# A DiT block pair on one Trainium2 core: a written order around the router, and a first gather for two expert pairs

## The chip, the cores and the metric

The kernel runs on one core of a Trainium2 chip. The core has five engines with instruction streams of their own: TensorE (PE) for matmuls, VectorE (DVE), ScalarE (ACT), GpSimd (POOL) and SyncE (SP), which here issues most of the weight loads. Sixteen DMA engines move the data. The metric is the device time of one execution in microseconds, the median of several runs.

## The reference

Two layers of a diffusion transformer work on 256 positions of x and 256 of a context, D = 1024, all in float32. Both layers take shift, scale and gate rows from a conditioning vector (`adaln`: a 1024 x 6144 matrix per layer). Layer 0 mixes with a gated linear attention and a spatial gating unit, projects back with `w_out` and ends with a mixture of experts on all 512 rows; layer 1 is a latent attention with the same mixture on the 256 rows of x. Around the change the layer reads:

```python
x = x + gate * (mix @ w_out)                     # residual of the mixer
h = modulate(rmsnorm(x, g), shift, scale)        # input of the router and of the experts
logits = h @ w_r + b_r                           # 4 group logits, 4 x 8 expert logits
# one softmax over groups and a top-2 softmax inside the chosen group: two experts per row
x = x + gate * sum_e weight_e * (silu(h Wg_e) * (h Wu_e)) Wd_e      # 32 experts, M_FF = 512
```

The gated linear attention, the latent attention and the rotary angles are not touched and are left out here.

## The kernel before

512 rows are four tiles of 128 tokens, `xs[0..3]` (0 and 1 are x, named `xx`; 2 and 3 the context, named `w` in the trace). A float32 product is done as three products of rounded halves, `mm3` (lines 120 to 122): a high and a low part of each operand, made by `split` (ACT copies the high part at line 115, DVE subtracts at line 116).

**Output projection (pool `out0`).** The mixer's result is multiplied with `w_out` in two halves of 512 columns. For the second half the loop `for t in range(4)` splits the weight into `WH` and `WL` (only at t = 0), does the 24 matmuls of tile t, and adds the gated result to `xs[t]` (`residual`, lines 776 and 777). `ada_next` computes a chunk of the conditioning rows of layer 1: 32 matmuls (L399, x64 in the trace) with 4 for the bias (L407), an ACT copy, and four small DMAs from the POOL queue into the DRAM tensor `mod`. Four chunks are left when the projection's second half begins.

**Router.** `R.half` and `R.tile` take the sum of squares, the inverse root (`rsqrt`, lines 95 to 101), turn the tile with 8 transposes (L213), and form 40 logits with 8 matmuls (L217) and one DVE instruction (L218, `lg`). `R.rows` makes the modulated rows: DVE multiplies with the broadcast row `rA` (L229), POOL adds the broadcast row `rS` (L230), then `split` writes them as `hH0`, `hL0`, `hH1`, `hL1`. `rA` and `rS` are 512 KB broadcast loads from `mod`, two of each, issued from ACT's queue. `R.route(0, 3)` and then `R.route(3, 4)` choose the experts: a chain of some forty small DVE steps (lines 248 to 302) that makes the mask `Mb`, PE's prefix sums over tokens (L277, L279), the positions `cm` (L281) and the weights `wsel`.

All engines but PE in the experts' part follow a scheduler that takes the ready instruction of highest priority; the order it finds is fixed in each engine's stream. On the projection PE too is ordered by it.

**Experts (`moe`).** Experts are handled in 16 pairs, up to 64 rows for each expert. For two pairs at a time, a one-hot matrix `P` (L856, 128 x 4 tiles x 256) selects the rows: `gather` (L881) multiplies the tokens with `P` and writes `xT`, transposed rows. A step of one pair is: two gate-and-up products (L916, `gu`, 16 matmuls for each expert; a float32 matmul is two in the trace, so x64 for both), `hidden` on ACT and DVE, `turned` (L935), `back` (L901), `down` (L1027, `dn`), and, delayed by a step, `combine` (L1046), which puts results back. PE runs this under a written order (`tc.manual_schedule`). The first gather is for one pair (128 columns of `P`); the other 128 columns are gathered inside step 0, between the second `gu` and `turned`. Later gathers are for two pairs at once, 256 columns. Between the first gather and the first `gu` stand four matmuls of `R.blocks` (L309), which lead to the count `nx` (L316), whose value SP reads before it goes on with loads; an overflow loop, which is not entered here, depends on it.

The weights of the experts, 12 MB a pair, come in 1 MB pieces through SP's queue (L849) into 13 buffers in layer 0 and 17 in layer 1; a load waits until PE has finished with what its buffer held.

Of the kernel before, what the change touches and what calls it, by code (L numbers as in the profile page):

```python
# [6 lines left out]
F32 = mybir.dt.float32  # L7
# [18 lines left out]
def body(ctx, tc, I, out, dbg=None, stop=None):  # L26
# [60 lines left out]
    def rsqrt(ss, n, inv, base=None):  # L87
# [9 lines left out]
        act(y, y, AF.Exp, scale=-0.5)  # L97
        V.tensor_tensor(a, y, y, op=OP.mult)
# [39 lines left out]
    class Router:  # L138
# [63 lines left out]
        def tile(self, t):  # L202

            cp, Q, c = self.cp, self.Q, t // 2
            ss = sm.tile([128, 1], F32, name="ss", bufs=4)
            act(junk_of(512), xs[t][:, 512:1024], AF.Square, accum_out=ss)
            rstd = rsqrt(ss, 1, 1.0 / D, self.v0[:, t:t + 1])
# [7 lines left out]
            pl = Q("bt")  # L215
# [3 lines left out]
            return rstd  # L219

        def rows(self, t, rstd, hs, A=None, S=None):
# [11 lines left out]
            split(h2, hs[:, 0, :], hs[:, 1, :])  # L233

        def route(self, t0, t1):
# [38 lines left out]
            prk = Q("bt", (128, 4, 32))  # L274
            for i in range(NT):
                t = t0 + i
                mm(prk[:, i, :], before, Mb[:, t, :], start=i == 0, stop=t == 0, skip_group_check=True)  # L277
                for u in range(t):
                    mm(prk[:, i, :], ones, Mb[:, u, :], start=False, stop=u == t - 1, skip_group_check=True)  # L279
            cm = self.cm[:, ts]  # L280
            V.scalar_tensor_tensor(cm, prk[:, 0:NT, :], 1.0, Mb[:, ts], op0=OP.add, op1=OP.mult)  # L281

            ge = small([4], "gex")
            V.tensor_tensor(ge, lg[:, :, 0:4], m1[:, :, 0:1].to_broadcast([128, NT, 4]), op=OP.subtract)
            act(ge, ge, AF.Exp)
            gs, gmax = small([1], "gs"), small([1], "gmax")
            V.tensor_reduce(gs[:, :, 0], ge, axis=AX.X, op=OP.add)
            V.tensor_reduce(gmax[:, :, 0], ge, axis=AX.X, op=OP.max)
            V.reciprocal(gs, gs)
            V.tensor_tensor(gs, gs, gmax, op=OP.mult)  # L290
            w1, w2, hw = small([5], "w1"), small([5], "w2"), small([5, 8], "l3")
            V.tensor_tensor(w2, m2, m1, op=OP.subtract)
            act(w2, w2, AF.Exp)
            V.tensor_scalar(w1, w2, 1.0, None, op0=OP.add)
            V.reciprocal(w1, w1)
            V.tensor_tensor(w1, w1, gs.to_broadcast([128, NT, 5]), op=OP.mult)
            V.tensor_tensor(w2, w1, w2, op=OP.mult)
            for h, w in ((hb, w1), (h2, w2)):
                src = h1 if h is hb else h2
                V.tensor_tensor(h.rearrange("p t g e -> p (t g) e"), src.rearrange("p t g e -> p (t g) e"),  # L300
                                w.rearrange("p t g -> p (t g)")[:, :, None].to_broadcast([128, NT * 5, 8]), op=OP.mult)
            V.tensor_tensor(fl(hw), fl(hb), fl(h2), op=OP.add)
            chosen(self.wsel[:, ts], hw)
# [28 lines left out]
    def even_layer(HL, main):  # L332
# [6 lines left out]
        with ExitStack() as st:  # L339
# [53 lines left out]
            def ada_chunk(l, c, w, cols=None):  # L393

                g, half = divmod(c, 2)
                pa = P("ad")
                for k in range(KC):
                    for j in range(4):
                        mm(pa[32 * j:32 * j + 32, 0:128], cst[:, k, :], w[k // 4][:, k % 4, j * 128:(j + 1) * 128],  # L399
                           start=k == 0, stop=cols is not None and k == KC - 1, skip_group_check=True)  # L400
                r = ap.tile([128, 128], F32, name="ada_r", bufs=2)
                if cols is not None:
                    act(r, pa[:, 0:128], AF.Copy)
                    tp(cols[:, c, :], r, ident)
                    return
                for j in range(4):
                    mm(pa[32 * j:32 * j + 2, 0:128], sbi[:, l * 12 + c, :], adab[:, j * 128:(j + 1) * 128],  # L407
                       start=False, stop=True, skip_group_check=True)
                if (l, g) in gains:
# [76 lines left out]
            def ada_next():  # L486
                ada_chunk(*adaq.pop(0))
                ada_ahead()
# [274 lines left out]
        with ExitStack() as st:  # L763
# [20 lines left out]
            rows, w, WH, WL = {}, ahead[0], [], []  # L784
            for t in range(4):
                c = t // 2
                if t % 2 == 0:
                    rows[c] = (bcast_row(cp, mod[0, 4, c], D, "rA"), bcast_row(cp, mod[0, 3, c], D, "rS"))
                acc = P("mm")
                for k in range(KC):  # L790
# [4 lines left out]
                    mm3(acc, tok(cH, k, t), tok(cL, k, t), WH[k], WL[k], k == 0, k == KC - 1)  # L795
                R.half(t)
                residual(t, 1, acc)
                rstd = R.tile(t)
                if t == 3:
                    R.route(0, 3)  # L800
                    R.route(3, 4)
                R.rows(t, rstd, HL.tile([128, 2, D], F32R, name=("hH0", "hL0", "hH1", "hL1")[t]), *rows[c])
# [7 lines left out]
    def moe(R, wxa, nwb, out=None):  # L810
# [5 lines left out]
        with ExitStack() as st:  # L816
# [301 lines left out]
            def step(p):  # L1118
# [70 lines left out]
    def odd_layer(HL, main):  # L1189
        rs = main.enter_context(tc.tile_pool(name="rs1", bufs=1, reuse_waits="tile"))  # L1190
        with ExitStack() as st:
# [194 lines left out]
            with tc.tile_pool(name="rt1", bufs=1, reuse_waits="tile") as R.cp, \  # L1386
# [35 lines left out]
                R.route(0, 2)  # L1422
# [57 lines left out]
```

## Time and profile before

| | us |
|---|---|
| median of 3 runs | 1553.11 |
| lowest, highest | 1551.04, 1554.37 |
| the profiled execution | 1554.18 |
| its span in the trace | 1552.40 |
| PE busy | 1459.8 (94%) |
| DVE, ACT, POOL busy | 664.9, 434.0, 225.3 |

The profile is of one execution. Its time is 1.78 us more than the span in the trace. Times in the trace count from the span's start. PE is busy for 94% of the span, but that is not the same as saying that PE sets the end: in parts it runs at half clock, and in parts the transfers set the pace. The stages are: projections and the mixer of layer 0 up to about 330 us, the second half of the output projection with the router up to 389, the experts of layer 0 from 389 to about 899, the latent attention up to 1075, and the experts of layer 1 to the end. The clock column of a window gives the granted TensorE clock as a share of 2.4 GHz; 0.50 is 1.2 GHz.

### The profile page before, as it was taken

How to read it: one execution, taken by the hardware profiler on the slowest of the kernel's cores; microseconds unless marked ns; L12 is line 12 of the kernel's file. 1: busy time of each engine (PE TensorE's matmuls, PEld its weight loads, DVE VectorE, ACT ScalarE, POOL GpSimd, SP SyncE). 2: the span in 40 equal slices, each digit the busy share in tenths (PEclk: the TensorE clock that was granted, in tenths of full speed). 3: DMA queues.
4: the chain of work that ended last, by engine and by line, in shares of the span. 5: the costliest groups of instructions: out<-in, count | busy, mean ns of one | idle time of the engine just before them, and what ended most of it. 6: DMA issues, size and time to landing. Idle time of an engine off the chain costs nothing. (4 is left out here: it accounts for less than half of the span.)

```text
span 1552.4 us, 21816 instructions
## 1 busy us (share of the span) xinstructions
PE 1459.8 (94%) x8622; PEld 857.8 (55%) x8622; DVE 664.9 (43%) x1498; ACT 434.0 (28%) x988; POOL 225.3 (15%) x250
## 2 busy tenths in 40 slices
PE   7999999998999999999999988997999989989987
PEld 5777777867644554554535356786344434444443
DVE  4555556758224334244413455576232332322222
ACT  4433334623121121111112144453222212212212
POOL 2321212133002112012203221101010100010010
PEclk9999999998799999999999989997999999999999
DMA  9774434885899999999999853125999999999994
GB/s 356 232 256 143 156 120 161 299 318 192 320 372 420 420 420 420 420 420 420 382 376 382 321 216 112 43 96 204 372 420 420 420 419 421 420 420 421 420 420 191
DMA packets 126052, 495.24 MB, mean 319 GB/s; under 512 B 17739, under 2 KB 38636, under 8 KB 77816
## 3 DMA queue, kind: packets, MB, share of 16 engines
q1 hardware_dynamic: 119704, 487.33, 79.6%
q10 hardware_dynamic: 2192, 3.72, 0.7%
q0 software_dynamic: 4048, 2.73, 0.6%
q8 instruction: 71, 1.16, 0.3%
q14 instruction: 37, 0.30, 0.1%
HBM read 492.59 MB, written 1.13 MB: 318 GB/s over the span
## 5 line engine op out<-in xcount | busy, mean ns | idle before, releaser
L916 PE MATMUL gu<-w,xT 128*64 128x512 f32 x2048 | 462.9, 604 | 18.0 <-DMA w<-in_moe_w_gu_dram 13.2
L916 PEld LDWEIGHTS gu<-w,xT 128*64 128x64 f32 x2048 | 153.3, 139 | 316.9 <-issue 278.5
L1027 PE MATMUL dn<-w,hh 128*64 128x512 f32 x960 | 219.5, 604 | 0.0
L924 DVE COPY hh<-gu 128x256 f32<-128x256 f32 x64 | 27.2, 425 | 371.3 <-ACT junk L923 371.3
L1050 POOL TENSOR_TENSOR xx<-xx,z 128x512 f32<-128x512 f32 x56 | 72.9, 1324 | 767.4 <-DVE z L1049 767.4
L1027 PEld LDWEIGHTS dn<-w,hh 128*64 128x64 f32 x960 | 76.1, 139 | 121.9 <-issue 112.3
L923 ACT ACTIVATE junk<-gu 128x256 f32<-128x256 f32 x64 | 24.6, 384 | 401.7 <-PE gu L916 401.7
L120 PE MATMUL mm<-WH,hH 128*128 128x512 f32 x288 | 116.7, 407 | 0.8 <-ACT hH L115 0.7
L121 PE MATMUL mm<-WL,hH 128*128 128x512 f32 x288 | 115.2, 400 | 1.4 <-DVE WL L116 1.4
L122 PE MATMUL mm<-WH,hL 128*128 128x512 f32 x288 | 112.5, 400 | 0.0
L1017 DVE SCALAR_TENSOR_TENSOR y<-dn,ws,y 128x512 fp32r<-128x512 f32 x60 | 45.0, 751 | 145.7 <-ACT y L1016 143.6
L1046 PE MATMUL ad<-y,PT 128*128 128x512 f32 x368 | 94.8, 404 | 5.3 <-DVE z L1049 4.1
L1016 ACT ACTIVATE y<-dn,ws 128x512 fp32r<-128x512 f32 x60 | 41.2, 687 | 176.1 <-PE dn L1027 165.6
L1046 PEld LDWEIGHTS ad<-y,PT 128*128 128x128 f32 x368 | 66.0, 188 | 36.1 <-issue 13.0
L115 ACT ACTIVATE WH<-w 128x512 fp32r<-128x512 f32 x80 | 48.4, 627 | 107.6 <-PE mm L122 86.0
L116 DVE TENSOR_TENSOR WL<-w,WH 128x512 fp32r<-128x512 f32 x76 | 56.6, 752 | 50.9 <-ACT WH L115 49.4
L1049 DVE TENSOR_TENSOR z<-ad,gt 128x512 f32<-128x512 f32 x100 | 66.1, 683 | 13.3 <-PE ad L1046 10.2
L881 PE MATMUL ad<-P,hH 128*128 128x256 f32 (+1 forms) x288 | 63.0, 302 | 1.5 <-DVE P L856 1.5
L120 PEld LDWEIGHTS mm<-WH,hH 128*128 128x128 f32 x288 | 54.9, 191 | 16.9 <-issue 3.8
L399 PE MATMUL ad<-w,cst 128*32 128x128 f32 x1536 | 59.3, 280 | 5.1 <-DMA w<-in_ada_w_dram 5.0
L121 PEld LDWEIGHTS mm<-WL,hH 128*128 128x128 f32 x288 | 54.8, 190 | 13.1 <-DVE WL L116 1.5
L122 PEld LDWEIGHTS mm<-WH,hL 128*128 128x128 f32 x288 | 54.5, 191 | 13.2 <-issue 1.6
(434 smaller groups left out, 1989.3 us busy)
## 6 DMA issues: line engine op xcount, KB each, us to landing
w<-in_moe_w_gu_dram SPq DMA_DIRECT2D x256, 1024.0 KB, 16.3
w<-in_moe_w_dn_dram SPq DMA_DIRECT2D x120, 1024.0 KB, 12.0
w<-in_ada_w_dram SPq DMA_DIRECT2D x48, 1024.0 KB, 7.4
w<-in_ev_w_in_dram SPq DMA_DIRECT2D x32, 256.0 KB, 4.6
w<-in_moe_w_dn_dram SPq DMA_DIRECT2D x16, 512.0 KB, 11.2
w<-in_ev_w_in_dram SPq DMA_DIRECT2D x6, 1024.0 KB, 5.1
w<-in_ev_w_out_dram SPq DMA_DIRECT2D x4, 1024.0 KB, 6.8
w<-in_od_w_out_dram SPq DMA_DIRECT2D x4, 1024.0 KB, 5.0
```

What stands on the lines that cost most here:

```text
L115: act(H, src, AF.Copy)
L116: (eng or V).tensor_tensor(L, src, H, op=OP.subtract)
L120: mm(out, lh, rh, start=start, stop=False, skip_group_check=True)
L121: mm(out, lh, rl, start=False, stop=False, skip_group_check=True)
L122: return mm(out, ll, rh, start=False, stop=stop, skip_group_check=True)
L399: mm(pa[32 * j:32 * j + 32, 0:128], cst[:, k, :], w[k // 4][:, k % 4, j * 128:(j + 1) * 128], start=k == 0, stop=cols is not None and k == ...
L881: mm(px[:, j, :], hs[t][:, part, 256 * (k // 2) + k % 2:256 * (k // 2) + 256:2], P[:, t, :], start=i == 0, stop=i == 2 * NT - 1)
L916: mm(gu[64 * c:64 * c + 64, :], xT[:, k, base:base + CAP], w[:, c], start=k == 0, stop=k == KC - 1)
L1027: mm(py[c][64 * par:64 * par + 64, :], hT[par][:, k // 2, k % 2, :], w_[par][:, k % 2, c * 512:(c + 1) * 512], start=k == 0, stop=k == 3)
L1046: mm(cb, PT[:, t, :], y[c][:, i % 2], start=i == 0, stop=i == 2 * len(pend) - 1)
L1049: V.tensor_tensor(z, cb, gate[t // 2][:, hs_], op=OP.mult)
L1050: (V if n % 4 == 3 else nc.gpsimd).tensor_tensor(xs[t][:, hs_], xs[t][:, hs_], z, op=OP.add)
```

## The change

1. From the projection's second half to the placement of the rows (`place`), PE, DVE and ACT run in a written order. The tile loop is cut into pieces: `project(t, k0, k1)` does half of a tile's 24 matmuls, `R.square`, `R.turn`, `R.logits` and the generator `R.rows` are called one by one. The four conditioning chunks, cut into `ada_chunk` (PE) and `ada_out` (the copy and the DMAs), get fixed places.
2. The addition of `rS` goes from POOL to DVE (line 245 of the changed kernel), and `rA` and `rS` are issued from POOL's queue in place of ACT's.
3. `route(0, 3)` and `route(3, 4)` become one `choose(0, 4)`, `place(0, 4)`, and `rest()`, which computes the weights. Layer 1 gets `choose(0, 2)`, `place` and `rest` too.
4. The first gather takes all 256 columns of `P`, and the gather inside step 0 is gone, in both layers. The making of `P` gets a high priority.

The core of the diff:

```diff
-            nc.gpsimd.tensor_tensor(h2, h2, S, op=OP.add)
+            yield
+            V.tensor_tensor(h2, h2, S, op=OP.add)
+            def mod_rows(c):
+                rA[c], rS[c] = (bcast_row(cp, mod[0, i, c], D, n, eng=nc.gpsimd) for i, n in ((4, "rA"), (3, "rS")))
...
+            mod_rows(0)
+            rstd, rows, xT = {}, {}, {}
+            with tc.manual_schedule(engines={mybir.EngineType.PE, mybir.EngineType.DVE, mybir.EngineType.Activation}):
+                project(0, 0, 4)
+                sums = ada_chunk(*adaq.pop(0))
+                project(0, 4, KC)
+                R.half(0)
+                ada_out(*sums)
+                ada_ahead()
+                for t in range(4):
+                    if t < 3:
+                        R.half(t + 1)
+                        if t < 2:
+                            project(t + 1, 0, 4)
+                    residual(t, 1, acc[t])
+                    if t:
+                        rows[t - 1] = rows_of(t - 1)
+                        next(rows[t - 1])
+                    ss = R.square(t)
+                    rstd[t] = rsqrt(ss, 1, 1.0 / D, R.v0[:, t:t + 1], (lambda: next(rows[t - 1])) if t else None)
+                    if t == 3:
+                        R.logits(2, rstd[2], xT[2])
+                    xT[t] = R.turn(t)
+                    if t:
+                        next(rows[t - 1])
+                        next(rows[t - 1], None)
+                    if t == 2:
+                        mod_rows(1)
+                    if t < 2:
+                        project(t + 1, 4, KC)
+                        R.logits(t, rstd[t], xT[t])
+                        if t == 1:
+                            sums = ada_chunk(*adaq.pop(0))
+                            ada_ahead(wpa)
+                            project(3, 0, 4)
+                            ada_out(*sums)
+                    elif t == 2:
+                        project(3, 4, KC)
+                rows[3] = rows_of(3)
...
+                rest = R.choose(0, 4)
+                next(rows[3])
+                next(rows[3], None)
+                R.place(0, 4)
...
+            rest()
...
-                elif p == 0:
-                    gather(P[:, :, 128:256], xT[:, :, 128:256])
...
-            P = one_hots(0)
+            with tc.high_priority():
+                P = one_hots(0)
...
-                gather(P[:, :, 0:128], xT[:, :, 0:128])
+                gather(P, xT)
```

What the diff leaves open is how the streams stand after it. On PE, where the second half of the projection begins, the stream before reads (`one` belongs to a column sum for the router, `w,cst` and `adab,sbi` to the conditioning chunks, `WH`, `WL` to the projection):

```order
L399 MATMUL ad<-w,cst 32x128 x32
L407 MATMUL ad<-adab,sbi 2x128 x4
L190 MATMUL bt<-s_3408,one 128x40
L399 MATMUL ad<-w,cst 32x128 x32
L120 MATMUL mm<-WH_3450,hH_3070 128x512
L407 MATMUL ad<-adab,sbi 2x128 x2
L120 MATMUL mm<-WH_3450,hH_3070 128x512
L407 MATMUL ad<-adab,sbi 2x128 x2
L190 MATMUL bt<-s_3417,one 128x40
L121 MATMUL mm<-WL_3451,hH_3070 128x512
```

And in the changed kernel, from the same place to the middle of tile 0:

```order
L192 MATMUL bt<-s_3408,one 128x40
L192 MATMUL bt<-s_3417,one 128x40
L122 MATMUL mm<-WH_3452,hH_3070 128x512
L123 MATMUL mm<-WL_3453,hH_3070 128x512
...
L123 MATMUL mm<-WL_3474,hH_3070 128x512
L124 MATMUL mm<-WH_3473,hL_3072 128x512
L434 MATMUL ad<-w,cst 32x128 x32
L437 MATMUL ad<-adab,sbi 2x128 x4
L122 MATMUL mm<-WH_3517,hH_3070 128x512
```

The two chunks that stood in front of the projection are gone from there: one now stands in the middle of tile 0, the next between tiles 2 and 3, the last two behind the logits of tile 3. Both column sums stand ahead of the first projection matmul.

On DVE, the end of the router before (the second chain, of tile 3 alone, with the numbers 383x to 387x) and the making of `P`:

```order
L264 TENSOR_TENSOR hb_3837<-h_3839,h_3847 128x40
L297 TENSOR_TENSOR w_3871<-w_3870,w_3871 128x5
L269 TENSOR_TENSOR Mb<-hb_3837,h_3839 128x32
L300 TENSOR_TENSOR h_3847<-h_3847,w_3871 128x40
L300 TENSOR_TENSOR hb_3837<-h_3839,w_3870 128x40
L302 TENSOR_TENSOR l_3872<-hb_3837,h_3847 128x40
L281 SCALAR_TENSOR_TENSOR cm<-bt,Mb 128x32
L269 TENSOR_TENSOR wsel<-l_3872,h_3839 128x32
L856 TENSOR_TENSOR P<-iota,cm 128x1024
```

In the changed kernel, the last logits and the additions of `rS` in front of the chain, and what stands between `Mb` and `P`:

```order
L251 TENSOR_TENSOR hH_3823<-h_3824,hH_3823 128x1024
L243 SCALAR_TENSOR_TENSOR h_3866<-w,rs_y,rA 128x1024
L233 SCALAR_TENSOR_TENSOR lg<-bt,rs_y,bS_3418 128x40
L245 TENSOR_TENSOR h_3866<-h_3866,rS 128x1024
L288 TENSOR_REDUCE m_3959<-lg 128x20
...
L298 TENSOR_TENSOR Mb<-hb_3962,h_3964 128x32 x4
L251 TENSOR_TENSOR hL_3865<-h_3866,hL_3865 128x1024
L322 TENSOR_TENSOR h_3972<-h_3972,w_4014 128x160
L322 TENSOR_TENSOR hb_3962<-h_3964,w_4013 128x160
L262 SCALAR_TENSOR_TENSOR cm<-bt,Mb 128x128
L324 TENSOR_TENSOR l_4015<-hb_3962,h_3972 128x160
L298 TENSOR_TENSOR wsel<-l_4015,h_3964 128x32 x4
L946 TENSOR_TENSOR P<-iota,cm 128x1024
```

One chain over 160 elements stands where two chains, of 120 and of 40, ran into each other. The addition of `rS` for tile 3 stands ahead of the chain, and the subtraction of `split` between `Mb` and `cm`.

On PE, from the first gather to the second pair, before:

```order
L881 MATMUL ad<-P,hH_3705 128x128 x2
L881 MATMUL ad<-P,hL_3883 128x128 x2
...
L309 MATMUL bt<-Mb,ones 128x32
L916 MATMUL gu<-w,xT 64x512 x32
L881 MATMUL ad<-P,hH_3551 128x128 x2
L881 MATMUL ad<-P,hL_3625 128x128 x2
```

and in the changed kernel, up to the first `gu` of the second pair:

```order
L971 MATMUL ad<-P,hL_3865 128x256 x2
...
L333 MATMUL bt<-Mb,ones 128x32
L1006 MATMUL gu<-w,xT 64x512 x32
L1025 MATMUL bt<-ident,hh 128x128 x4
L991 MATMUL bt<-ident,z 128x128 x4
L1117 MATMUL dn<-w,hh 64x512 x16
L1006 MATMUL gu<-w,xT 64x512 x32
```

The 64 matmuls of the first gather have 256 columns in place of 128, and the 64 that stood between the second `gu` and `turned` (L935 before, L1025 now) are gone; nothing stands in their place. On POOL's queue the issues of `rA` and `rS` stand, for the first pair, ahead of the additions of the first residual half, and for the second pair behind the `mod` writes of the first two chunks.

## Rows read from the trace of the kernel before

**Rows 1.** Page, part 4: the chain that ended last, by line, in its second row.

```profile
DMA w<-in_moe_w_gu_dram 9%; DMA w<-in_moe_w_dn_dram 5%; PE gu L916 1%; PE dn L974 0%; PE dn L1027 0%; PE ad L1046 0%; PE ad L958 0%; DVE xT L992 0%; PE bt L134 0%; DVE hh L927 0%; PE ad L961 0%; ACT xT L998 0%; PE bt L935 0%; DVE z L1033 0%; PE ad L988 0%
```

**Rows 2.** Windows: stretch, length, busy time by engine, granted clock, DMA share, GB/s.

```profile
390.00:400.00 10.00, 10.00 (x49) 10.00 (x49) 0.69 (x1) 0.00 (x0) 0.54 (x1) 0.50 0.93 385
400.00:410.00 10.00, 10.00 (x47) 5.08 (x48) 1.61 (x5) 0.60 (x1) 0.00 (x0) 0.75 0.34 109
...
440.00:500.00 60.00, 59.77 (x312) 29.46 (x308) 22.85 (x37) 11.42 (x26) 8.17 (x6) 1.00 1.01 420
...
1080.00:1090.00 10.00, 10.00 (x43) 6.18 (x45) 2.97 (x9) 1.83 (x4) 0.00 (x0) 0.62 0.06 18
```

**Rows 3.** Waits of SP's queue from 400 to 800 us: total, times, longest.

```profile
SPq L849 <- PE dn L1027: 178.3, 25, 12.8
```

**Rows 4.** Timeline of PE, start of the projection's second half and its end.

```profile
330.49 1.96 PE L399 MATMUL ad<-w,cst 128*32 128x128 f32 x64
...
338.69 0.51 PE L121 MATMUL mm<-WL,hH 128*128 128x512 f32 x1 [1.38 <-DVE WL L116]
...
365.64 0.39 PE L121 MATMUL mm<-WL,hH 128*128 128x512 f32 x1
365.86 0.40 PE L122 MATMUL mm<-WH,hL 128*128 128x512 f32 x1
```

**Rows 5.** Timeline of DVE, the modulated rows of tiles 0 and 1.

```profile
355.77 1.28 DVE L229 SCALAR_TENSOR_TENSOR h<-xx,rs_y,rA 128x1024 f32<-128x1024 f32 x1
...
357.16 3.46 DVE L229 SCALAR_TENSOR_TENSOR h<-xx,rs_y,rA 128x1024 f32<-128x1024 f32 x1
```

**Rows 6.** Timeline of DVE, from the last logits to the one-hot matrix.

```profile
380.38 0.25 DVE L218 SCALAR_TENSOR_TENSOR lg<-bt,rs_y,bS 128x40 f32<-128x40 f32 x1
380.55 0.27 DVE L248 TENSOR_TENSOR h<-l,m 128x120 f32<-128x120 f32 x1
...
387.43 1.22 DVE L856 TENSOR_TENSOR P<-iota,cm 128x1024 fp32r<-128x1024 f32 x1
```

**Rows 7.** DMA issues from 340 to 440 us: queue, count, size, median time to landing.

```profile
gt<-mod POOLq DMA_DIRECT2D x2, 512.0 KB, 7.8
```

**Rows 8.** Timeline of PE, first gather to the second pair's gate-and-up.

```profile
388.70 0.69 PE L881 MATMUL ad<-P,hH 128*128 128x128 f32 x2 [1.54 <-DVE P L856]
...
402.69 15.09 PE L916 MATMUL gu<-w,xT 128*64 128x512 f32 x64
...
427.34 7.09 PE L1027 MATMUL dn<-w,hh 128*64 128x512 f32 x32
434.26 2.31 PE L916 MATMUL gu<-w,xT 128*64 128x512 f32 x10
```

**Rows 9.** Window inside a later gather, instructions of L881 alone (PE, PEld, clock, DMA).

```profile
508.00:514.00 6.00, 5.75 (x48) 5.58 (x47) 1.00 1.02 421
```

**Rows 10.** Timeline of PE, a run of 256-column matmuls in the latent attention.

```profile
948.28 0.58 PE L121 MATMUL mm<-wL,kvH 128*128 128x256 f32 x1 [0.37 <-POOL wL L116]
...
950.79 0.41 PE L120 MATMUL mm<-wH,kvH 128*128 128x256 f32 x1
...
951.91 0.28 PE L122 MATMUL mm<-wH,kvL 128*128 128x256 f32 x1
```

**Rows 11.** Timeline of PE, the first pair behind the overflow check.

```profile
787.94 0.51 PE L935 MATMUL bt<-ident,hh 128*128 128x128 f32 x2
...
792.94 9.35 PE L1027 MATMUL dn<-w,hh 128*64 128x512 f32 x32
802.12 1.45 PE L916 MATMUL gu<-w,xT 128*64 128x512 f32 x6
```

**Rows 12.** Timeline of PE, first gather and first pair of layer 1.

```profile
1077.37 7.09 PE L881 MATMUL ad<-P,s 128*128 128x128 f32 x32 [1.43 <-DVE P L856]
...
1084.47 3.94 PE L916 MATMUL gu<-w,xT 128*64 128x512 f32 x10
```

**Rows 13.** Window of the projection of tile 0 with a low clock.

```profile
340.20:343.40 3.20, 3.20 (x9) 2.50 (x8) 3.20 (x8) 0.00 (x0) 2.02 (x4) 0.50 1.07 421
```

More of the change, by code (lines that the diff above doesn't have):

```diff
@@ L214, in tile, with logits @@
                 act(xT[:, kk * 4:kk * 4 + 4, :], p, AF.Copy)
-            pl = Q("bt")
+            return xT
+        def logits(self, t, rstd, xT):
+            c, pl = t // 2, self.Q("bt")
             for k in range(KC):
@@ L272, in route @@
             chosen(Mb[:, ts], hb)
[L274 to L291, printed above, removed]
@@ L305, in blocks @@
+            return rest
         def blocks(self, cp, Q):
@@ L399, in ada_chunk, with ada_sums @@
                         mm(pa[32 * j:32 * j + 32, 0:128], cst[:, k, :], w[k // 4][:, k % 4, j * 128:(j + 1) * 128],
-                           start=k == 0, stop=cols is not None and k == KC - 1, skip_group_check=True)
+                           start=k == 0, stop=k == KC - 1, skip_group_check=True)
                 r = ap.tile([128, 128], F32, name="ada_r", bufs=2)
[L402 to L405, printed above, removed]
+                act(r, pa[:, 0:128], AF.Copy)
+                tp(cols[:, c, :], r, ident)
+            def ada_sums(l, c, w, pa):
+                for k in range(KC):
+                    for j in range(4):
+                        mm(pa[32 * j:32 * j + 32, 0:128], cst[:, k, :], w[k // 4][:, k % 4, j * 128:(j + 1) * 128],
+                           start=k == 0, stop=False, skip_group_check=True)
                 for j in range(4):
@@ L408, in ada_chunk, with ada_out @@
                        start=False, stop=True, skip_group_check=True)
+                return l, c, pa
+            def ada_out(l, c, pa):
+                g, half = divmod(c, 2)
+                r = ap.tile([128, 128], F32, name="ada_r", bufs=2)
                 if (l, g) in gains:
@@ L783, in even_layer, with project @@
                 residual(t, 0, acc0[t])
[L784 to L790, printed above, removed]
+            w, WH, WL, acc = ahead[0], [], [], {}
+            rA, rS = {}, {}
+            def mod_rows(c):
+                rA[c], rS[c] = (bcast_row(cp, mod[0, i, c], D, n, eng=nc.gpsimd) for i, n in ((4, "rA"), (3, "rS")))
+            def project(t, k0, k1):
+                if k0 == 0:
+                    acc[t] = P("mm")
+                for k in range(k0, k1):
                     if t == 0:
@@ L794, in even_layer @@
                         split(w[k // 4][:, k % 4, :], WH[k], WL[k])
[L795 to L802, printed above, removed]
+                    mm3(acc[t], tok(cH, k, t), tok(cL, k, t), WH[k], WL[k], k == 0, k == KC - 1)
@@ new lines, in rows_of @@
+            def rows_of(t):
+                return R.rows(t, rstd[t], HL.tile([128, 2, D], F32R, name=("hH0", "hL0", "hH1", "hL1")[t]), rA[t // 2], rS[t // 2])
+            mod_rows(0)
[38 more added lines that the diff above has]
+                next(rows[3])
+                sums = ada_chunk(*adaq.pop(0)) if adaq else None
+                R.logits(3, rstd[3], xT[3])
+                next(rows[3])
+                if sums:
+                    ada_out(*sums)
+                    sums = ada_chunk(*adaq.pop(0)) if adaq else None
+                rest = R.choose(0, 4)
+                next(rows[3])
+                next(rows[3], None)
+                R.place(0, 4)
+                if sums:
+                    ada_out(*sums)
@@ L803, in even_layer @@
+            assert not adaq and not todo
+            rest()
             while adaq:
@@ L1421, in odd_layer @@
                     rstds.append(R.tile(t))
-                R.route(0, 2)
+                rest = R.choose(0, 2)
+                R.place(0, 2)
+                rest()
                 for t in range(2):
-                    R.rows(t, rstds[t], HL.tile([128, 2, D], F32R, name=f"s{t}"))
+                    for _ in R.rows(t, rstds[t], HL.tile([128, 2, D], F32R, name=f"s{t}")):
+                        pass
         return R
```

69 lines of the change are left out of this document (50 added, 19 removed).

## The prediction, made before the changed kernel ran

> **What bounds the kernel now.** I read the windows by stage first, then the waits of the load queue, then the chain that ended last, and only then the timelines of the places that the change touches.
>
> In the experts of layer 0 PE is busy 59.77 of 60 us at full clock, beside a DMA share of 1.01 [rows 2]. Both look full, and the queue's waits decide: from 400 to 800 us SP waits 178.3 us for `dn` matmuls, that is, for buffers that PE still holds [rows 3]. So PE sets the pace there, and a microsecond saved on PE before 440 moves the whole stage, provided the loads can come earlier too. They can: from 400 to 410 the DMA share is only 0.34 [rows 2], and 13 buffers are filled ahead. In layer 1 the chain that ended last is the weight loads, with every PE line at 1% or less [rows 1]. There a saving on PE counts only where it starts the stream earlier; the stream stands nearly still from 1080 to 1090, at a share of 0.06 [rows 2].
>
> The stretch of the change itself lies on one path: projection, last logits, choice, `P`, first gather, first pair. From 390 to 400 PE is 10.00 of 10.00 busy, and so is its weight load, but the clock is 0.50 [rows 2]: 1.2 GHz. The first gather takes from 388.70 to 402.69, with four small matmuls 13.99 us, and the first `gu` begins at that clock [rows 8].
>
> **The written order up to `P`.** Before, the first projection matmul with `WL` comes at 338.69, after a wait for DVE, and tile 3 ends at 366.26; two chunks of 1.96 us (about 2.35 with their bias matmuls) stand ahead of it [rows 4]. Now these two stand inside, 4.7 us; the start gains less, since the order waits for both column sums and for DVE's first `WL`: I estimate 337.1 for the start, so tile 3 ends 3.1 us later, at 369.4.
>
> Behind it the path is shorter. Before, the last logits come at 380.38, 14.1 us after the projection, and `P` starts 7.05 us later [rows 6]. Part of these 14.1 us is contention: one DVE instruction with `rA` takes 1.28 us alone and 3.46 when POOL adds `rS` beside it [rows 5]. With the addition on DVE, four instructions of about 1.2 us come onto DVE, 4.9 us, but those stretched by POOL shrink: 2.2 us for the one of tile 1. Counting the instructions of the new DVE order with 1.2 to 1.3 us for each of 128x1024, 0.3 for each 160-wide step (0.27 at 120 wide [rows 6]) and 0.1 for small ones: 1.4 for the residual, 1.3 + 1.2 for tile 2's row, 1.2 + 1.3 for its split and tile 3's product, 0.3 + 1.2 for logits and addition, 5.1 for the chain up to `Mb`, 2.6 for the subtraction, weights and `cm`, 1.2 for `P`: 16.8, and 1.8 for waits on ACT between them. `P` would be done at 388.0, against 387.43 + 1.22 = 388.65 before.
>
> `rA` and `rS` of the second pair come through POOL's queue now, behind tile 1's use of the old rows (one buffer each). I take them issued at about 364 and wanted at about 371. The nearest row is another 512 KB broadcast from POOL: 7.8 us to landing, in full traffic [rows 7]. So DVE waits 0 to 3 us, with all of the written order behind it; I take 1.2. The net shift of `P` is +0.5, with bounds of -2 and +4.
>
> On this the Trainium skill's page "DMA: Bandwidth & Descriptors", section "Anatomy of one DMA — SWDGE (gpsimd) path", gives a fit of 2.0 us plus bytes over 436 GB/s, an estimate of 3.2 us for 512 KB. By that the rows would never be late and the term would be -0.7; the measured 7.8 us decides, and with it the +0.5 stands.
>
> **The first gather.** The number of matmuls stays at 64; each has 256 columns. At half clock a 256-column matmul goes every 0.21 us: twelve from 948.28 to 950.79 [rows 10], which is the pace of the old gather too, 64 in 13.7 us [rows 8]. At full clock it is 5.75 us for 48, 0.12 each [rows 9]. So the second half of the columns is free, and what matters is when the clock comes back. Of those twelve in the latent attention the next ones are shorter, 0.28 against 0.41 [rows 10]: the clock rose after 2.5 us. The `dn` of the pair behind the overflow check took 9.35 us in place of 7.09, so it ran some 4.5 us at half clock [rows 8, 11]. With 3.6 us between: 17 matmuls at 0.21 and 47 at 0.12 make 9.2, against 13.7: -4.5 (bounds -5.0 and -4.0 if it rises; 0 if not). The first `gu` then runs at full clock: before it had 0.50 up to about 405.0, since the window from 400 to 410 has a mean of 0.75 [rows 2], which cost half of 2.3 us: -1.2.
>
> **The tail of step 0.** `gu` ends at 402.69 + 15.09 = 417.78, and the next pair's begins at 434.26: 16.5 us [rows 8], of which the second gather, 64 matmuls at 0.12 [rows 9], is 7.7. What it covered is late next: the second expert's activation, and the copies behind `turned`. The nearest row is the pair behind the overflow check, which has the same sequence without gather and combine: 787.94 to 802.12, 14.18 us, with a fall of the clock in its waits that made `dn` 2.26 longer [rows 11]. That is -2.3; without the fall it would be 11.9, -4.6. Since the waits are for the same instructions, I take the row with its fall, and -2.2, a tenth less, for a wait on the next `P`'s place in DVE's order.
>
> **Layer 1.** Its gather of 32 matmuls takes 7.10 us at half clock [rows 12]; with a rise after 3.4 it is 15 x 0.22 + 17 x 0.12 = 5.4, -1.7. The first `gu` then frees its first weight buffer at full clock: another -1.7. One more load stands ahead of SP's read of `nx` than before, so the stream starts with the freed buffer and not with `nx`. I take -3.0 of these 3.4 for the stream (bounds -1, if `nx` holds it, and -4). The second gather's removal gives nothing there, since loads set the pace.
>
> **The sum.** +0.5 - 4.5 - 1.2 - 2.2 - 3.0 = -10.4. The profiled execution took 1554.18, so 1543.8; the median lies 1.07 below that execution, so I predict 1542.7. The likeliest case's own range, from the bounds of the terms, is 1537 to 1549.
>
> **Rivals.**
>
> *The clock does not come back inside the gather.* For it speaks that 13.7 us of uninterrupted matmuls in the old gather did not raise it [rows 2, 8]; against it the 2.5 us in the latent attention, with 256 columns as here [rows 10]. Then the gather stays at 13.7, `gu` begins slow as before, layer 1 gains at most 0.5, and the sum is +0.5 - 2.2 - 0.5 = -2.2: 1550.9.
>
> The Trainium skill's page "TensorE: Matmul & The Clock Gate", section "Part 1: The HAM clock gate", says that the throttled state is the default and that activity releases it. By that rule alone the old gather should have risen too; the trace does not agree (0.50 over all of 390 to 400 [rows 2]), so I leave this rival a chance.
>
> *PE waits in the written order.* Before, a ready matmul of another tile filled each gap. Now PE stands at each turn and each logits until DVE and ACT are done: five such places inside the projection. Half a tile's 12 matmuls, 0.22 us apart [rows 4], cover 2.7 us, and the residual is 1.4 of that; the rival decides where DVE has over 1.3 us of other work ahead of the residual, a single row instruction being 1.2 to 1.3 [rows 5]. One wait costs what the wait of 1.38 cost: it and 3.2 us at half clock behind it [rows 4, 13], 1.4 + 1.6 = 3.0, or 3.7 with the longer return of the `dn` above. Five make 15 to 18.5; with the gains behind `P` the sum is about +6.5: 1559.5. It is slower from four or five waits on. Against it: each tile's rows are placed behind the next half projection.
>
> *No fall in step 0's tail.* If the shorter gather and the DVE order leave no gap long enough, the tail gives -4.6, and if `P` also comes 2 us early, the sum is -15.3: 1537.8. For it speaks that the wait before `turned` is about 2 us; against it the row with the fall.
>
> *The order does not do what it says, the queue holds it:* the second `rA` and `rS` late by the full bound of +4 give 1546.2; that lies inside the likeliest case's range.
>
> **How the numbers follow.** The likeliest case has 0.68, the clock rival 0.12, the waits 0.11, the better tail 0.09. A difference of 0.2%, 3.1 us, is about what a measurement of this kernel tells from no change: the bounds are 1550.0 and 1556.2. The clock rival falls within them, with a little of the likeliest case's upper edge: same 0.14. Slower is nearly all of the waits' rival, 0.10. Faster is the rest, 0.76. The range leaves out the worst of the waits and the best of the tail: 1536 to 1552.
>
> **What would show it.** Right: the first gather's matmuls go from 0.21 to 0.12 apart some 3 to 4 us after the first; its end comes near 398.5; `gu` takes 13.7; from its end to the next `gu` 12 to 14.5 us; POOL shows no addition of `rS`; the first load of layer 1's new stream comes 3 us earlier, against the end of layer 0, than before. `P` stands within 2 us of 388.6. Wrong: a gather at 0.50 throughout; PE waits of over a microsecond, several of them, between tiles of the projection; a DVE wait for `rA`; or a stage of layer 0's experts whose PE now waits for weights, so that what is won before 440 is given back there.

## The result, and the profile after

| | before | changed |
|---|---|---|
| median of 6 runs, us | 1553.1 | 1544.99 |
| lowest, highest | 1551.04, 1555.69 | 1543.07, 1547.97 |
| profiled execution, its span | 1554.18, 1552.40 | 1543.41, 1541.60 |

The ratio is 0.9948, with a 95% interval of 0.9933 to 0.9962: 8.1 us faster, 5.9 to 10.4. I had predicted 1542.7 in 1536 to 1552, that is, 10.4 below the kernel before. The sum was near, but two of its terms were wrong by 3.0 and 3.5 us, in opposite directions.

Before two traces are compared, a word on the part where nothing was changed. Up to the last matmul of the projection's first half the instructions of PE, DVE, ACT and POOL come in the same order in both kernels (only the loads of the broadcast rows are issued elsewhere), yet that matmul ends at 330.56 before and at 332.74 after: PE waited longer for a weight load near 85 us (3.90 us after, 2.25 before). The end of this first half is therefore the zero from which I count below.

The start of the projection's second half on PE in the changed kernel (timeline: start, length, engine, line, tiles, and in brackets the idle time and what ended it), against [rows 4]:

```profile
336.12 0.62 PE L192 MATMUL bt<-s,one 128*128 128x40 f32 x2 [3.38 <-DVE s L190]
338.51 0.62 PE L192 MATMUL bt<-s,one 128*128 128x40 f32 x2 [1.76 <-DVE s L190]
340.31 0.77 PE L122 MATMUL mm<-WH,hH 128*128 128x512 f32 x1 [1.18 <-DVE ymix L811]
...
345.70 2.20 PE L434 MATMUL ad<-w,cst 128*32 128x128 f32 x64
...
365.64 1.88 PE L232 MATMUL bt<-wA,h2T 128*128 128x40 f32 x16
...
372.53 1.05 PE L225 MATMUL bt<-ident,w 128*128 128x128 f32 x8
...
375.94 0.39 PE L124 MATMUL mm<-WH,hL 128*128 128x512 f32 x1
```

Three waits, 6.3 us, stand where the two chunks stood before: for the first column sum, for the second, and for the PSUM buffer that the first half's gate product frees. Behind them the clock is low; a window of the same trace shows it:

```profile
340.30:345.70 5.40, 5.39 (x12) 3.78 (x12) 5.40 (x8) 1.45 (x4) 2.91 (x2) 0.50 0.67 239
```

From there to the end of tile 3, 376.33, PE has no wait at all. Tile 3 ends 43.6 us after the first half, where it was 35.7 before (366.26 - 330.56). The two chunks stand inside this stretch in both kernels, so they are not the difference. PE waits 4.5 us more (6.3 against 1.8), and the logits of tile 1 and the turn of tile 2 (365.64 and 372.53 above), some 2.5 us, now stand ahead of tile 3's end; before, they came behind it:

```profile
366.98 1.98 PE L217 MATMUL bt<-wA,h2T 128*128 128x40 f32 x16
368.79 1.12 PE L213 MATMUL bt<-ident,w 128*128 128x128 f32 x8
```

DVE behind the projection in the changed kernel, against [rows 5, 6]:

```profile
378.73 1.28 DVE L243 SCALAR_TENSOR_TENSOR h<-w,rs_y,rA 128x1024 f32<-128x1024 f32 x1 [0.94 <-DMA rA<-mod]
...
384.85 0.25 DVE L233 SCALAR_TENSOR_TENSOR lg<-bt,rs_y,bS 128x40 f32<-128x40 f32 x1
385.01 1.21 DVE L245 TENSOR_TENSOR h<-h,rS 128x1024 f32<-128x1024 f32 x1
...
393.62 1.22 DVE L946 TENSOR_TENSOR P<-iota,cm 128x1024 fp32r<-128x1024 f32 x1
```

`rA` is late by 0.94 us, and `P` starts 60.9 us after the first half, against 56.9: 17.3 us behind the end of tile 3, against 21.2. The stretched instruction of 3.46 us has no counterpart any more; all with `rA` take 1.28.

The first gather and step 0 on PE, against [rows 8]:

```profile
394.89 0.79 PE L971 MATMUL ad<-P,hH 128*128 128x256 f32 x2 [3.44 <-DVE P L946]
...
400.18 0.63 PE L971 MATMUL ad<-P,hH 128*128 128x256 f32 x2
400.61 0.53 PE L971 MATMUL ad<-P,hL 128*128 128x256 f32 x2
400.97 0.40 PE L971 MATMUL ad<-P,hH 128*128 128x256 f32 x2
...
405.48 13.95 PE L1006 MATMUL gu<-w,xT 128*64 128x512 f32 x64
419.37 0.51 PE L1025 MATMUL bt<-ident,hh 128*128 128x128 f32 x2
421.94 0.50 PE L1025 MATMUL bt<-ident,hh 128*128 128x128 f32 x2 [2.06 <-DVE hh L1017]
423.19 0.66 PE L991 MATMUL bt<-ident,z 128*128 128x128 f32 x4 [0.75 <-ACT hh L1029]
423.77 7.09 PE L1117 MATMUL dn<-w,hh 128*64 128x512 f32 x32
430.69 9.61 PE L1006 MATMUL gu<-w,xT 128*64 128x512 f32 x44
```

A row here is two matmuls. They get shorter, 0.63 to 0.40, at 400.6: the clock came back 5.7 us into the gather, which takes 10.6 us to `gu` where it was 13.99. `gu` is 13.95 (15.09 before). From its end, 419.43, to the next pair's `gu` it is 11.3 us (16.5 before), and the second half of `turned` waits 2.06 us for `hh`, yet `dn` has its full speed.

Layer 1, PE, against [rows 12]:

```profile
1071.92 6.20 PE L971 MATMUL ad<-P,s 128*128 128x256 f32 x32 [1.43 <-DVE P L946]
...
1078.11 13.96 PE L1006 MATMUL gu<-w,xT 128*64 128x512 f32 x64
```

And the windows, against [rows 2]:

```profile
440.00:500.00 60.00, 59.70 (x310) 29.52 (x308) 23.08 (x38) 11.42 (x26) 8.18 (x6) 1.00 1.01 420
...
1080.00:1090.00 10.00, 10.00 (x50) 3.32 (x48) 2.35 (x8) 1.22 (x3) 0.00 (x0) 1.00 0.86 328
```

In the experts of layer 0 nothing is given back: PE is as busy as before, and the load queue still waits 163.3 us for `dn` from 400 to 800 us (178.3 before [rows 3]). The window from 1080 to 1090 can't be set against the same one before, since layer 1 begins 5.5 us earlier now. It begins 9.8 us behind the first placement matmul of layer 1; from there the kernel before has

```profile
1085.45:1095.45 10.00, 10.00 (x44) 3.17 (x42) 2.49 (x9) 1.67 (x4) 0.00 (x0) 0.89 0.60 238
```

so the stream of loads is at 0.86 where it was at 0.60. The load queue's wait for the count `nx` in layer 1 (1050 to 1130 us) is gone, before and after:

```profile
SPq L1178 <- DVE nx L316: 21.3, 1, 21.3
```

```profile
SPq L1267 <- DVE nx L340: 0.6, 1, 0.6
```

Counted from the first placement matmul of layer 1 (1075.63 before, 1070.18 after), the end comes after 476.8 us before and 471.4 after.

### The profile page after: what moved, and what is told of

It reads as the page before. It is cut to its first block, busy times and chain, and to the rows that moved or that the text cites. A ratio compares the mean times of both kernels' runs of the same rounds, so it can differ in the third digit from the quotient of the medians.

```text
span 1541.6 us, 21585 instructions
## 1 busy us (share of the span) xinstructions
PE 1434.2 (93%) x8526; PEld 836.9 (54%) x8526; DVE 659.1 (43%) x1472; ACT 432.5 (28%) x982; POOL 217.6 (14%) x250
## 5 line engine op out<-in xcount | busy, mean ns | idle before, releaser
L1006 PE MATMUL gu<-w,xT 128*64 128x512 f32 x2048 | 458.3, 599 | 20.8 <-DMA w<-in_moe_w_gu_dram 13.7
L118 DVE TENSOR_TENSOR WL<-w,WH 128x512 fp32r<-128x512 f32 x76 | 55.1, 730 | 54.0 <-ACT WH L117 53.5
L1139 DVE TENSOR_TENSOR z<-ad,gt 128x512 f32<-128x512 f32 x100 | 66.1, 682 | 13.5 <-PE ad L1136 10.3
L122 PEld LDWEIGHTS mm<-WH,hH 128*128 128x128 f32 x288 | 55.0, 191 | 18.6 <-issue 5.5
L449 POOL DMA_DIRECT2D mod<-ada_r x80 | 40.4, 512 | 157.0 <-ACT ada_r L447 128.7
L971 PE MATMUL ad<-P,hH 128*128 128x256 f32 x256 | 54.7, 296 | 3.4 <-DVE P L946 3.4
```

Of the source, the lines that this page charges most:

```text
L118: (eng or V).tensor_tensor(L, src, H, op=OP.subtract)
L122: mm(out, lh, rh, start=start, stop=False, skip_group_check=True)
L971: mm(px[:, j, :], hs[t][:, part, 256 * (k // 2) + k % 2:256 * (k // 2) + 256:2], P[:, t, :], start=i == 0, stop=i == 2 * NT - 1)
L1006: mm(gu[64 * c:64 * c + 64, :], xT[:, k, base:base + CAP], w[:, c], start=k == 0, stop=k == KC - 1)
L1139: V.tensor_tensor(z, cb, gate[t // 2][:, hs_], op=OP.mult)
```

## The experiments

The changed kernel has two parts that can be taken apart: the written order, and the gather. Two opposed theories stood after the traces. M: the gather earns everything and the order costs some 4 us, because PE idles where the chunks were taken away. O: the order itself earns part of the gain, or the gather needs it. The runs come from several chips; so each time is given with its ratio to the kernel before on the same chip, and in us against 1553 by that ratio. Each kernel has one profile, and the same stream can differ there: with the changed kernel's order, tile 3 ends 41.9 to 44.0 us after the first half in three traces, and with the chunks in front 37.2 to 38.9 in four.

**The gather alone.** The kernel before with:

```diff
-                elif p == 0:
-                    gather(P[:, :, 128:256], xT[:, :, 128:256])
-            P = one_hots(0)
+            with tc.high_priority():
+                P = one_hots(0)
-                gather(P[:, :, 0:128], xT[:, :, 0:128])
+                gather(P, xT)
```

> The kernel before, with the first gather for two pairs and without step 0's second gather, in both layers; no written order on DVE and ACT, rS added on POOL, rA and rS from ACT's queue. Theory M (the gather earns all, the written order costs some 4 us because PE idles where the projection starts): P starts within 1 us of 57 us after the last matmul of the projection's first half, as before; gather -3.5, first gu -1.1, tail -2.3 to -5.2, layer 1 -4: 1540 to 1543 us, faster than the changed kernel by 2 to 5. Rival O (the order is needed for the gain): 1546 to 1550.

Measured: 1541.29, ratio 0.9928 (0.9908 to 0.9948), -11.2 us. `P` starts 57.9 us after the first half, 1.1 later than before. The tail of its step 0:

```profile
400.48 13.95 PE L916 MATMUL gu<-w,xT 128*64 128x512 f32 x64
...
418.77 8.78 PE L1027 MATMUL dn<-w,hh 128*64 128x512 f32 x32
427.38 1.03 PE L916 MATMUL gu<-w,xT 128*64 128x512 f32 x4
```

From `gu`'s end to the next it is 12.95 us here, with a slow `dn`. Theory O falls: the gather does not need the order.

**The order alone.** The changed kernel with the two gathers of before in both layers (the diff above, backwards).

> The changed kernel with the gathers of before (128 columns first, the other 128 inside step 0) in both layers. Theory M: P starts 60 to 61 us after the last matmul of the projection's first half, 4 later than before, the gather stays at 13.7 us, and the time is 1553 + 4 = 1557 (1555.5 to 1558.5). Rival O: the order earns by itself, 1550 or less. If both parts add, e1 plus e2 less before is the changed kernel's time, 1545.

Measured: 1555.56, ratio 1.0020 (1.0005 to 1.0035), +3.1 us. `P` starts 61.3 us after the first half. So the order costs, as theory M said, though the interval only just leaves out no change. The two parts add within the intervals: -11.2 + 3.1 = -8.1, the changed kernel's own -8.1.

**The two chunks in front again.** The changed kernel with:

```diff
             mod_rows(0)
+            ada_next()
+            ada_out(*ada_chunk(*adaq.pop(0)))
+            ada_ahead(wpa)
...
                 project(0, 0, 4)
-                sums = ada_chunk(*adaq.pop(0))
                 project(0, 4, KC)
                 R.half(0)
-                ada_out(*sums)
-                ada_ahead()
...
-                            sums = ada_chunk(*adaq.pop(0))
-                            ada_ahead(wpa)
                             project(3, 0, 4)
-                            ada_out(*sums)
```

> The changed kernel, but the two conditioning chunks stand in front of the projection again, as before, and not inside it. Theory M (PE's idle 6.3 us in front of the projection is empty because these chunks, 4.7 us, were taken out of it): tile 3's projection ends 4 to 5 us earlier against the first half's end (43.6 us after it in the changed kernel), P too, and the time is 1541 (1539.5 to 1542.5). Rival W (DVE's order behind the projection or the rows rA sets P's time): P moves by less than 1.5 us and the time stays at 1544 to 1546.

Measured: 1537.28, ratio 0.9905 (0.9885 to 0.9925), -14.8 us. The same place on PE:

```profile
332.87 1.95 PE L434 MATMUL ad<-w,cst 128*32 128x128 f32 x64
...
335.68 0.39 PE L192 MATMUL bt<-s,one 128*128 128x40 f32 x2 [0.53 <-DVE s L190]
336.00 1.96 PE L434 MATMUL ad<-w,cst 128*32 128x128 f32 x64
...
339.48 0.47 PE L122 MATMUL mm<-WH,hH 128*128 128x512 f32 x1 [0.56 <-DVE ymix L811]
339.79 0.39 PE L123 MATMUL mm<-WL,hH 128*128 128x512 f32 x1
```

The waits for the first column sum and the PSUM buffer are 0.5 and 0.6 in place of 3.4 and 1.2, the second column sum is not waited for (1.8), the matmuls behind are at 0.39 and not at 0.63, tile 3 ends 37.2 us after the first half, and `P` starts at 53.5: 7.4 earlier than in the changed kernel, and 3.4 earlier than before. That is more than the 4 to 5 us of theory M, which counted the chunks alone: up to tile 3's end PE waits 2.6 us and not 6.3, it does not run at half clock there, and `rA`, issued earlier, is not late. So the written order is good behind the projection's start: `P` comes 16.3 us behind tile 3's end, where it was 21.2 before. What made it a loss was what it took away from the start.

**The addition of rS back on POOL**, on the kernel of the last experiment (one line: `nc.gpsimd.tensor_tensor(h2, h2, S, op=OP.add)`).

> The kernel of e3_chunks_first with the addition of rS on POOL, as before. Theory (DVE and POOL slow each other, one 1.28 us instruction took 3.46 beside it): P comes 1 to 3 us later than 53.5 after the first half's end: 1538.3 to 1540.3. Rival (four instructions of 1.2 us less on DVE, which is the path behind the projection): P 1 to 2.5 us earlier: 1535 to 1536.3.

Measured: 1541.43, ratio 0.9931 (0.9912 to 0.9950), 4.1 us worse than with it on DVE by the ratios, whose intervals overlap a little. The traces are clearer: `P` starts 57.3 us after the first half in place of 53.5, more than the theory's 1 to 3 us, and 19.9 us behind tile 3's end in place of 16.3. Two additions on POOL (374.06 to 376.43, and 380.06 to 382.41), and two small instructions of DVE that ran into them:

```profile
374.06 2.37 POOL L245 TENSOR_TENSOR h<-h,rS 128x1024 f32<-128x1024 f32 x1 [4.76 <-ACT rs_y L97]
...
380.06 2.35 POOL L245 TENSOR_TENSOR h<-h,rS 128x1024 f32<-128x1024 f32 x1
```

```profile
374.22 2.23 DVE L101 TENSOR_TENSOR rs_a<-rs_a,rs_v 128x1 f32<-128x1 f32 x1
...
380.53 2.06 DVE L277 TENSOR_TENSOR h<-lg,m 128x160 f32<-128x160 f32 x1
```

Elsewhere they take 0.16 and 0.33. In each of the four additions the first TENSOR_TENSOR that DVE began inside it ended only with it, within 0.2 us, even where it is one element wide (1.91, 1.92, 2.23 and 2.06 us). A TENSOR_REDUCE that began at 380.18, inside the last one, took 0.32, as without. With the addition on POOL `P` stands where it stood before (57.3, 56.9), so the move to DVE is what makes the order gain its 3.4 us.

**Tile 3's subtraction not between `Mb` and `cm`**, on the kernel with the chunks in front: `R.place(0, 4)` stands ahead of the last `next(rows[3], None)`, which the scheduler places.

> The kernel of e3_chunks_first with the subtraction of tile 3's split no longer written between Mb and cm, but left to the scheduler. Theory: it stands on the path with 1.2 us, so P starts 1.2 earlier after Mb (4.2 us in the changed kernel's trace between the end of Mb's chain and P's end becomes 3.0) and the time is 1536 (1534.5 to 1537.5). Rival: it moves into the chain in front of Mb, and P stands where it stood, 53.5 us after the first half's end: 1537.3.

Measured: 1537.24, ratio 0.9916 (0.9900 to 0.9931), no difference. From `Mb` to `P` it is 1.86 us (383.78 to 385.64) in place of 2.99 (390.63 to 393.62 in the changed kernel), but `P` starts 53.9 us after the first half, as without. The subtraction went into the chain in front of `Mb`, the rival's case: DVE has no wait there, and it makes no difference on which side of `Mb` this instruction stands.

**The gate products ahead of the splits**, on the same kernel: `residual(0, 0, ...)` and `residual(1, 0, ...)` written in front of `project(0, 0, 4)`, the other two behind it.

> The kernel of e3_chunks_first with the first half's gate products of tiles 0 and 1 (ymix) written ahead of the splits of WL, since the projection of tile 0 waited for the PSUM buffer that they free (1.18 us in the changed kernel's trace). Theory: PE starts tile 0 1 to 2.5 us earlier than 6.5 us after the first half's end, tile 3 ends as much earlier, and the time is 1535 to 1536.3. Rival: WL is late by the same 1.3 us and sets the start, or the gate rows, whose load is on the way, do: no change or later, 1537 to 1538.5.

Measured: 1544.34, ratio 0.9955 (0.9938 to 0.9971), 7.8 us worse by the ratios. PE:

```profile
342.63 0.65 PE L192 MATMUL bt<-s,one 128*128 128x40 f32 x2
...
348.61 0.50 PE L123 MATMUL mm<-WL,hH 128*128 128x512 f32 x1 [0.94 <-DVE WL L118]
...
352.20 0.50 PE L123 MATMUL mm<-WL,hH 128*128 128x512 f32 x1 [2.63 <-DVE WL L118]
```

Now PE waits 3.6 us for `WL` in place of 0.8, the rival's case, and worse than it said: the second pair of gate products hands its additions to POOL while DVE makes the next `WL`, which are stretched (two in 4.27 us where two take 1.28). Tile 3 ends 45.1 us after the first half, 7.9 later than without. Half of that stands ahead of the projection, whose first matmul comes 10.5 us after the first half and not 6.5: PE waited 1.86 us for the weight of a conditioning chunk, and ran at half clock behind it. The next kernel has such a wait too (1.46 us) without this edit, so one profile does not show that this half belongs to it.

**Work for PE in the waits for `Mb` and `P`**, on the kernel with the chunks in front. The results of these matmuls are read by nobody:

```diff
+                warm = P("mm")
+                for i in range(18):
+                    mm(warm, WH[1][:, 0:128], WH[0], start=True, stop=True, skip_group_check=True)
                 rest = R.choose(0, 4)
...
+                for i in range(12):
+                    mm(warm, WH[1][:, 0:128], WH[0], start=True, stop=True, skip_group_check=True)
```

> The kernel of e3_chunks_first with 18 matmuls of 512 columns on PE behind the last conditioning chunk and 12 behind the placement, whose results nobody reads: extra work in the waits for Mb and P. Theory: the clock at the first gather is low because PE waited in front of it; with PE busy there it stays at 1.00, the gather goes at 0.12 us a matmul from the start (8.0 us up to gu in place of 9.2 to 10.6), step 0 gains nothing else: 1534 to 1536. Rival: the extra matmuls run at half clock, 0.43 us each, and the placement waits for them: P later by 2 us or more, 1538 to 1541.

Measured: 1530.93, ratio 0.9875 (0.9855 to 0.9896), -19.4 us. The extra matmuls at 384.29, then the gather:

```profile
384.29 2.99 PE L892 MATMUL mm<-WH,WH 128*128 128x512 f32 x12
387.89 0.52 PE L973 MATMUL ad<-P,hH 128*128 128x256 f32 x2 [0.61 <-DVE P L948]
388.25 0.40 PE L973 MATMUL ad<-P,hL 128*128 128x256 f32 x2
...
395.89 13.95 PE L1008 MATMUL gu<-w,xT 128*64 128x512 f32 x64
```

The gather runs at 0.12 us a matmul from its second row: 8.0 us up to `gu`. That explains 1.2 to 2.6 us against the kernels without, as the theory said. The extra matmuls do not hold `P` up: it comes 16.6 us behind tile 3's end, 16.3 without them. The rest of the 4.6 us by which this kernel beats the chunks alone is not explained, and lies beyond the theory's range. In these two traces the largest difference behind step 0 stands between the `dn` of the pair ahead of the overflow check and of the second pair behind it, 65.6 us here and 70.9 in the other, with the same instructions; the `dn` between them is 7.09 here and 9.27 there. But it is 7.09 too with the subtraction moved and with the gate products ahead, which have no such matmuls, so this difference is not shown to come from the change.

**The same in the tail of a step**: eight more such matmuls between the second `gu` and `turned`, where neither combine nor gather stands (step 0, and the pair behind the overflow check).

> The kernel of e6_warm with eight more unread matmuls of 512 columns, 1.9 us, between the second gate-and-up product and turned wherever no combine or gather stands there: in step 0 and in the pair behind the overflow check, in both layers. Theory (the fall of the clock in the tail of a step comes from PE's wait of 2.05 us before turned): dn takes 7.09 us in both places in layer 0 in place of 8.2 to 9.4, from gu's end to the next gu 11.0 to 11.6 us, and the time is 1528.5 to 1531, some 1 to 2 below e6_warm where that had the falls. Rival (the fall has its cause earlier, in the slow stretch ahead of the first gu or in the overflow check): dn stays at 8.2 or more in at least one of the two places: 1531 or more.

Measured: 1528.76, ratio 0.9866 (0.9844 to 0.9888), -20.8 us, the lowest of all, though its interval overlaps the one of the kernel without the eight. Step 0, and the pair behind the check:

```profile
409.10 2.12 PE L1241 MATMUL ad<-hH 128*128 128x512 f32 x8
...
411.67 0.50 PE L1027 MATMUL bt<-ident,hh 128*128 128x128 f32 x2 [0.22 <-DVE hh L1019]
...
413.51 7.09 PE L1119 MATMUL dn<-w,hh 128*64 128x512 f32 x32
...
777.01 7.09 PE L1119 MATMUL dn<-w,hh 128*64 128x512 f32 x32
```

`dn` has its full speed in both places, although the `gu` behind the check still began slowly (15.29). In step 0 `dn` was 8.2 to 8.8 us in the seven other kernels with the new gather, and 7.09 in the changed kernel's own profile. Behind the check it was 7.08 or 7.09 in four of the ten other traces, without any extra matmul in that pair. So the theory fits, but one profile does not show that the fall is cured; what the eight matmuls do take away is the wait before the second half of `turned`, 0.22 us in place of 2.06.

**Layer 1 with the old gathers**, the changed kernel otherwise (`if l:` the two gathers of before).

> The changed kernel with the gathers of before in layer 1 alone. Theory M (in layer 1 both the short first gather and the missing second one count, since the load stream starts earlier and does not stand still near the end of the first dn): 1545 + 4 to 5.5 = 1549 to 1550.5, and the dip of the DMA share about 20 us behind the stream's start is back. Rival S (the missing second gather gives nothing where loads set the pace, as I predicted): 1545 + 2 to 3 = 1547 to 1548, no dip.

Measured: 1547.40, ratio 0.9968 (0.9953 to 0.9983): layer 1's part is worth 3.1 us by the ratios, 2.4 by the medians, near rival S. From layer 1's first placement matmul to the end it is 477.5 us here, 476.8 before and 476.5 with the order alone; in the eight profiles with the new gather it is 470.2 to 474.4, mean 472.0, so 4.9 less by the traces, inside theory M's range. The load queue waits for `nx` again, 21.2 us. The dip of the load stream that I had looked for comes with both kinds: 5 us at a DMA share of 0.83 before and of 0.80 with the chunks in front. Whether the missing second gather counts beside the shorter first one is not decided.

In the same trace stands step 0 of layer 0, whose PE stream is the changed kernel's word for word:

```profile
420.31 0.71 PE L991 MATMUL bt<-ident,z 128*128 128x128 f32 x4 [0.75 <-ACT hh L1029]
420.95 8.68 PE L1117 MATMUL dn<-w,hh 128*64 128x512 f32 x32
```

The same waits, 2.06 and 0.75, and `dn` at 8.68 here, 7.09 there.

## Why the prediction was right

**What bounds the kernel: right.** What was won ahead of 440 us stayed: `dn` of the twelfth pair comes 326.2 us after that of the first in the changed kernel, 326.1 before.

**The written order up to `P`: wrong, the largest miss.** I had +0.5 with bounds of -2 and +4; measured from the end of the first half it is +4.0, and the order alone cost 3.1. The step that failed is "I estimate 337.1 for the start, so tile 3 ends 3.1 us later". Counted from the end of the first half, that start is 6.5 us, and it was 7.6; tile 3 ended 7.9 later. Of the 4.8 us that I missed, 1.0 is the start: I had counted the wait for the column sums and `WL`, but not that the two column sums come one after the other, nor the PSUM buffer as a third. About 1.0 is the clock: 12 matmuls in 5.4 us in place of 2.7, where the low clock of the kernel before had cost 1.6 [rows 13], and I had charged no more for the longer wait. The largest part, some 2.5, is work that I left out of the sum: the logits of tile 1 and the turn of tile 2 now stand inside the projection. The chunks put in front again gave 7.4 us back at `P`, through the waits, the clock and `rA`.

**From tile 3 to `P`: near, with luck in one term.** I counted 18.6 us from the projection's end to `P`'s, and 1.2 for a late `rA`, 19.8 together; it was 18.5 with a wait of 0.94 for `rA` in it. This wait came out near by two errors: `rA` was issued 4.8 us ahead of its use and not 7, and its landing took 5.8 us:

```profile
rA<-mod POOLq DMA_DIRECT2D x1, 512.0 KB, 5.8
```

This lies below the 7.8 that I took [rows 7]. The Trainium skill's page "DMA: Bandwidth & Descriptors", section "Anatomy of one DMA — SWDGE (gpsimd) path", gives by its fit an estimate of 3.2; the trace does not agree. With the chunks in front the same load took 3.8 us.

**The gather: right in kind, too small.** -4.5 expected; -3.4 in the changed kernel, where the clock came back after 5.7 us in place of my 3.6 and the gather took 10.6 us up to `gu`; in six of the others it took 9.2 to 10.3, with the clock back earlier (after 2.8 us in the shortest). The rival without a return falls: the clock came back in each of the seven traces where it had fallen, and with PE busy ahead of the gather it never left (1.00 from 370 to 396 us). The Trainium skill's page "TensorE: Matmul & The Clock Gate", section "Part 1: The HAM clock gate", says that activity releases the throttle; the busy waits agree with it, while the old gather, busy from 390 to 400 at 0.50 [rows 2], still does not.

**The first `gu`: right.** -1.2 expected, -1.1.

**The tail of step 0: too small.** -2.2 expected, -5.2 in this profile, -3.6 in the others. I had taken the row of the pair behind the check whole [rows 11]; there, `dn` was slowest of all, 9.35. The rival "no fall in step 0's tail" is what this one execution shows. That is luck: the same PE stream, with the old gathers in layer 1, had the fall.

**Layer 1: right within what can be told.** -3.0 expected; 2.4 to 3.1 by the runs, 4.9 by the traces. The mechanism that I named is there: the load queue no longer waits for `nx` (0.6 us in place of 21.3).

**The rival of the waits: its mechanism was there, at another place.** PE waited in the written order, but once, ahead of the projection, and not between the tiles, where the half projections covered DVE as planned. It cost 4 us and not 15, and left the sign as it was.

So the sum held in part by luck: +3.5 in the order stood against -3.0 in the tail of this profile; of the other terms the gather was off by 1.1, the first `gu` by 0.1, and layer 1 by 2.4 in this pair of traces. With the tail of the other profiles, -3.6, and 2.4 to 4.9 for layer 1, the measured terms add up to -6.5 to -9.0, and the runs give -8.1.

## What to carry to other kernels

A written order takes away what a scheduler would have put into a wait. Before work is moved out of a place, look at what stands there on that engine when it is gone: here 4.7 us of filler were moved from in front of a wait into a full stretch, and cost 7.4. Where PE must wait in front of a run of matmuls, unread matmuls in the wait can pay, as the clock then stays up: the gather behind them took 8.0 us in place of 9.2 to 10.6. A single profile of each kernel is not enough to price a fall of the clock. And when two traces are compared, count from a point ahead of the first difference.

## What was not expected of the hardware

The same PE stream with the same waits of 2.06 and 0.75 us had a `dn` of 7.09 us in one execution and of 8.68 in another; a price for a fall of the clock, taken from one row, was off by as much as that. Two executions of the same instructions stood 3 us apart from 90 us on, after one wait for a load (2.25 us in one, 3.90 in the other) and the low clock behind it. And an addition on POOL stretched a one-element instruction on DVE from 0.16 to 2.23 us.
